# The output product of a hybrid decoder layer: half of its contraction as seven products of sums of blocks, two row blocks at a time

## The chip, the core and the metric

The kernel runs on one core of one Trainium2 chip. The metric is the device time of an execution in microseconds (us). A core has five engines that run side by side and wait for one another through semaphores: TensorE (PE, matmuls; PEld its weight loads), VectorE (DVE, V in the code), ScalarE (ACT, S), GpSimd (POOL, G) and SyncE (SP), which here issues every DMA. Operands lie in SBUF, matmuls write to PSUM, which has eight banks of 128 x 512 float32; the large arrays lie in HBM.

## The reference

One layer of inference for a prompt of 1024 tokens and 32 sample tokens (8 sequences of 4), width 1024, float32. What matters here is its end:

```python
u = jax.nn.sigmoid(gm) * (y_m @ w_mo) + jax.nn.sigmoid(ga) * (y_a @ w_ao)
x = x + gate * (u @ w_o)
...
y_prompt = rmsnorm(yp, g_final)     # the same for the 32 sample rows
```

`u @ w_o` is the output product: 1024 (and 32) rows, a contraction over 1024, 1024 columns. After it every row is scaled by its gate, added to the residual x, and normed by its mean square.

## The kernel before

The layer runs in stages: norm and gates of the input, the input projection (most of it already as seven products of sums of blocks, `block_products`), attention and the matrix memory beside it, and at the end three products: `att_out` (y_a by w_ao), `mem_out` (y_m by w_mo), and the output product.

**Splitting.** A float32 operand is split into a high part (a cast to the matmul's reduced float32, on ScalarE) and a low part (the difference, on VectorE or GpSimd). A product of two operands is three matmuls: high by high, high by low, low by high.

**The w_mo product.** `for d in range(KT)` runs eight steps; step d makes 128 of the 1024 columns of u for all tokens, in three pieces of 384, 384 and 288 tokens. The pieces go through four PSUM banks in turn (`banks`: pg, pg, pa, pa), and VectorE empties them: `tgw_mo` is gated, then added to u (for d of 6 and 7 by GpSimd). Beside step d two halves of row block d of w_out are loaded (`raw`, 128 x 512), and split into `wo_h[d, i]` and `wo_l[d, i]`: the cast on ScalarE, the low part of one half on VectorE, of the other on GpSimd. All 32 halves stay in SBUF. They come from the pool `half` (`ht`), of 43 buffers; raw loads come from the pool `wr` of nine.

**The output product.** The loop runs over the eight row blocks of 128 tokens. A block's u (eight pieces of 128 x 128) is split, and for each half of the columns 24 matmuls of 128 x 512 (8 parts of the contraction, three each) are summed in one PSUM bank. The eighth block does its second half as two quarters of 256 columns. `add_part` multiplies the bank by the gate (`gbc`), adds it to the residual row `xb`, and has ScalarE square it with a running sum; `last_norm` forms the factor of the rows with eleven or so small steps on VectorE (`recip_sqrt`: a bit trick and three iterations) and scales and stores the two halves.

**The sample rows.** The 32 sample rows would use a quarter of TensorE's columns; `sample_rows` therefore runs four parts of the contraction side by side, on the unsplit w_out, which is loaded once more, sixteen halves of 256 KB (`wos`). It is a generator that the loop over row blocks resumes: eight matmuls for each half of the contraction and each half of the columns, sixteen in a go, then three additions on VectorE.

**Storage at the end.** `gbc` (gates of the prompt), `gsb` (of the samples), `gf` (final gain) and the residual rows are eight tiles of 128 x 1024, `misc`, in two quarters of SBUF (`l0`, `l1`) that hold y_m until the last matmul of the w_mo product.

**Order.** The instructions are ordered for each engine by a scheduler at build time, which works through what is ready, by place in the program; PE's order is the program's. `Ordered` ties the instructions of VectorE and ScalarE to the order written while its `on` is set; it is off from the middle of the kernel to the end. SP's queue works in order: a DMA that waits for its buffer holds back those behind it.

Of the kernel before, what the change touches and what calls it, by code (L numbers as in the profile page):

```python
# [10 lines left out]
F32 = mybir.dt.float32  # L11
# [9 lines left out]
D = 1024  # L21
# [151 lines left out]
def body(tc, a):  # L173
    nc = tc.nc
    with ExitStack() as ctx:
# [5 lines left out]
        def pg(shape, name):  # L181
            return ps.tile(shape, F32, tag="g", bufs=2, name=name)
# [4 lines left out]
        def pb(shape, name):  # L187
            return ps.tile(shape, F32, tag="b", bufs=2, name=name)
# [51 lines left out]
        def dma(out, in_, late=False):  # L240
            stores(in_.tensor)
            issue(out, in_, late)
# [10 lines left out]
        def mm(out, lhsT, rhs, start, stop, share=1, more=False):  # L253
            n = int(np.prod(rhs.shape[1:]))
            side.now += max(n, 250) / 2400 if rhs.dtype == F32R else max(n * 4 // share, 128) / 2400
            side.products += 1
            in_order(nc.tensor.matmul(out, lhsT, rhs, start=start, stop=stop, skip_group_check=more))  # L257
# [6 lines left out]
        def recip_sqrt(half, shape, name):  # L264

            yi = sm(shape, name + "_y", 2)
            w = sm(shape, name + "_w", 2)
            V.tensor_scalar(yi.bitcast(I32), half.bitcast(I32), 1, None, op0=ALU.logical_shift_right)
            V.tensor_scalar(yi.bitcast(I32), yi.bitcast(I32), -1, -0x2108A621, op0=ALU.mult, op1=ALU.add)
            for _ in range(3):  # L270
                if shape[1] == 1:
                    V.scalar_tensor_tensor(w, yi, half, yi, op0=ALU.mult, op1=ALU.mult)
                else:
                    V.tensor_tensor(w, yi, yi, op=ALU.mult)
                    V.tensor_tensor(w, w, half, op=ALU.mult)
                V.scalar_tensor_tensor(yi, w, 1.5, yi, op0=ALU.subtract, op1=ALU.mult)
            return yi
# [1499 lines left out]
        wo_h, wo_l = {}, {}  # L1777
        for d in range(KT):
            mem_out(d, ymx, u)
            for i in range(2):  # L1780
                raw = raw_tile(f"wo{d}_{i}").rearrange("p k n -> p (k n)")
                dma(raw, a["w_out"][d * 128:(d + 1) * 128, HALF[i]], True)
                wo_h[d, i], wo_l[d, i] = (ht([128, 512], f"wo_{x}{d}", F32R) for x in "hl")
                S.copy(wo_h[d, i], raw)
                (G if i else V).tensor_tensor(wo_l[d, i], raw, wo_h[d, i].bitcast(F32), op=ALU.subtract)


        assert not due
# [12 lines left out]
        def add_part(xb, src, gb, n, cf, ss):  # L1801
            t = ht([128, 512], "fot")[:n, :cf.stop - cf.start]
            V.tensor_tensor(t, src, gb[:n, cf], op=ALU.mult)
            V.tensor_tensor(xb[:n, cf], xb[:n, cf], t, op=ALU.add)
            jk = ht([128, 512], "fjk", BF16)
            S.activation(jk[:n, :cf.stop - cf.start], xb[:n, cf], AF.Square, accum_out=ss)

        def last_norm(tb, xb, n, ss, parts):
            v = sm([128, 1], "fv", 2)
            V.tensor_scalar(v[:n], ss[:n, 0:1], 0.5 / D, 0.5 * EPS, op0=ALU.mult, op1=ALU.add)  # L1810
            for f in range(1, len(parts)):
                V.scalar_tensor_tensor(v[:n], ss[:n, f:f + 1], 0.5 / D, v[:n], op0=ALU.mult, op1=ALU.add)
            r = recip_sqrt(v[:n], [n, 1], f"fr{n}")
            yo = a["y_p"][tb * 128:tb * 128 + 128] if tb < 8 else a["y_s"]
            lo, hi = slice(0, 512), slice(512, D)
            if tb == 7:
                V.tensor_tensor(xb[:n, lo], xb[:n, lo], gf[:n, lo], op=ALU.mult)
                S.activation(xb[:n, lo], xb[:n, lo], AF.Copy, scale=r)
            else:
                V.scalar_tensor_tensor(xb[:n, lo], xb[:n, lo], r, gf[:n, lo], op0=ALU.mult, op1=ALU.mult)  # L1820
            dma(yo[:, lo], xb[:n, lo])
            V.scalar_tensor_tensor(xb[:n, hi], xb[:n, hi], r, gf[:n, hi], op0=ALU.mult, op1=ALU.mult)
            dma(yo[:, hi], xb[:n, hi])

        def sample_rows():
            xb = residual(8, NS)
            acc = [po([128, 512], f"fo8_{f}") for f in range(2)]
            for kq in range(0, KT, 4):
                raws = []
                for k in range(kq, kq + 4):  # L1830
                    for f in range(2):
                        raws.append(raw_tile(f"wos{k}{f}").rearrange("p k n -> p (k n)"))
                        dma(raws[-1], a["w_out"][k * 128:(k + 1) * 128, HALF[f]])
                yield
                for f in range(2):
                    for j in range(4):
                        mm(acc[f][32 * j:32 * j + 32], u(kq + j, SEQ, NS), raws[2 * j + f],
                           start=(kq == 0), stop=(kq > 0))
            ss = sm([128, 3], "fsss", 1)
            for f in range(2):  # L1840
                yield
                t = ht([128, 512], "fo8s")[:NS]
                S.copy(t, acc[f][0:32])
                for j in (32, 64, 96):
                    V.tensor_tensor(t, acc[f][j:j + 32], t, op=ALU.add)
                add_part(xb, t, gsb, NS, slice(f * 512, f * 512 + 512), ss[:NS, f:f + 1])
            last_norm(8, xb, NS, ss, (0, 1))

        rows8 = sample_rows()
        for tb in range(8):  # L1850
            if 2 <= tb < 7:
                next(rows8, None)
            t0 = tb * 128
            xb = residual(tb, 128)
            uh, ul = [], []
            for k in range(KT):
                if k % 4 == 0:
                    gh, gl = (granule(f"u{tb}{t}{k}", t, 4, F32R) for t in ("wh", "wl"))
                us = u(k, t0, 128)
                uh.append(gh[:, k % 4])  # L1860
                ul.append(gl[:, k % 4])
                S.copy(uh[k], us)
                V.tensor_tensor(ul[k], us, uh[k].bitcast(F32), op=ALU.subtract)
            ss = sm([128, 3], "fss", 2)
            parts = ((0, 512), (512, 256), (768, 256)) if tb == 7 else ((0, 512), (512, 512))
            for f, (p0, pn) in enumerate(parts):
                cf = slice(p0, p0 + pn)
                acc = pg([128, 512], f"fo{tb}_{f}")
                o = acc[:, :pn]
                for k in range(KT):  # L1870
                    mm(o, uh[k], wo_h[k, p0 // 512][:, p0 % 512:p0 % 512 + pn], start=(k == 0), stop=False)
                    mm(o, uh[k], wo_l[k, p0 // 512][:, p0 % 512:p0 % 512 + pn], start=False, stop=False)
                    mm(o, ul[k], wo_h[k, p0 // 512][:, p0 % 512:p0 % 512 + pn], start=False, stop=(k == KT - 1))
                add_part(xb, o, gbc, 128, cf, ss[:, f:f + 1])
            last_norm(tb, xb, 128, ss, parts)


OUTS = {
# [73 lines left out]
```

## Time and profile before

| | us |
|---|---|
| median of 3 runs | 854.86 (854.39 to 855.19) |
| the profiled execution | 853.27 |
| its span, first to last instruction | 851.1 |
| PE busy in the span | 830.6 (98%) |
| DVE, ACT, POOL busy | 566.5, 387.8, 41.8 |
| w_mo product on the chain | 705.15 to 751.6 |
| output product on the chain | 751.6 to 843.25 |

Times inside the kernel are counted from the start of the span. In the rows of a timeline stand the start, the length, the engine, the line, the operation, its result and its operands, and in brackets how long the engine had been idle and what released it. In the rows of groups stand the count, the busy time, the mean in ns, and the idle time ahead. In the rows of stretches stand the length and the busy time of PE, PEld, DVE, ACT and POOL with the number of instructions, then the granted clock of TensorE, the busy share of the DMA engines and GB/s. The granted clock is 0.998 of full speed over the run. Line 219 is the helper of `Ordered`, line 257 that of every matmul, and line 245 that of every DMA issue, so the groups are told apart by tiles: `fo` is the output product's bank, `u0wh` to `u7wl` are the split row blocks, `rows_l` the residual rows, `fot` the gated part, `fjk` the squares, `fr_y` and `fr_w` the norm's factor.

### The profile page before, as it was taken

The page shows a single profiled execution, that of the slowest core. Times are in us where ns is not written, and L with a number is a line of the kernel's source. Part 1 is how long each engine was busy: PE and PEld are TensorE (multiplying, and loading weights), DVE is VectorE, ACT ScalarE, POOL GpSimd, SP SyncE. Part 2 cuts the span into 40 slices and gives each one's busy share as a digit, 9 for nine tenths or more (in the row PEclk, how much of TensorE's full clock was granted, in tenths as well). Part 3 has the DMA queues.
Part 4 walks back from the last instruction along what each step waited for, and adds up shares of the span by engine and source line. Part 5 has one row for each costly group of instructions (what it writes and reads, how often), then busy time and mean ns, then how long its engine had stood idle before and what let it go on. Part 6 is the DMA issues. An engine that isn't in the chain of part 4 may idle for free.

```text
span 851.1 us, 15314 instructions
## 1 busy us (share of the span) xinstructions
PE 830.6 (98%) x5256; PEld 697.7 (82%) x5256; DVE 566.5 (67%) x1600; ACT 387.8 (46%) x989; POOL 41.8 (5%) x81
## 2 busy tenths in 40 slices
PE   6899999999999999999999999999999999999996
PEld 3689989789888988888888777777778999987785
DVE  3787785555666785656655656787877657746586
ACT  4672356546665564555444444444446232223231
POOL 0220000000000000000000000000002011220000
PEclk9999999999999999999999999999999999999999
DMA  9996549348537565273423453554435789353402
GB/s 324 365 360 187 144 142 293 107 118 288 193 102 234 167 187 169 84 223 95 134 97 110 133 135 105 150 165 125 125 113 178 276 277 305 123 161 113 172 25 80
DMA packets 114321, 146.48 MB, mean 172 GB/s; under 512 B 27089, under 2 KB 70993, under 8 KB 114213
## 3 DMA queue, kind: packets, MB, share of 16 engines
q1 hardware_dynamic: 114244, 145.52, 53.3%
q8 instruction: 41, 0.67, 0.3%
q14 instruction: 36, 0.29, 0.1%
HBM read 107.50 MB, written 38.99 MB: 172 GB/s over the span
## 4 chain that ended last, share of the span: by engine, by line
PE 93%; ACT 2%; DVE 2%; DMA 1%; issue 1%; SPq 0%; DVEq 0%; ACTq 0%
PE fo L257 11%; PE bx L257 11%; PE by L257 10%; PE bw L257 10%; PE g_aq L257 6%; PE g_w_mo L257 5%; PE bz L257 5%; PE g_w_ao L257 5%; PE g_mq L257 4%; PE g_mk L257 3%; PE g_mv L257 3%; PE smp L257 2%; PE sc L257 2%; PE oT L257 2%; PE pt L262 1%; PE g_ak L257 1%
## 5 line engine op out<-in xcount | busy, mean ns | idle before, releaser
L257 PE MATMUL g_w_ao<-ya,wh_w_ao 128*128 128x384 f32 (+1 forms) x192 | 45.6, 322 | 0.1
L257 PE MATMUL g_w_mo<-ym_l,wh_w_mo 128*128 128x384 f32 (+1 forms) x192 | 45.7, 323 | 0.0
L219 ACT ACTIVATE p<-p,nmx 128x256 f32<-128x256 f32 (+1 forms) x64 | 31.0, 487 | 20.6 <-DVE nmx L219 20.6
L219 ACT ACTIVATE fjk<-rows_l 128x512 bf16<-128x512 f32 (+2 forms) x19 | 11.6, 609 | 50.3 <-DVE rows_l L219 26.3
L219 DVE CUSTOM_DVE_ANT_0 p<-sc,cst,sink 128x256 f32<-128x256 f32 (+1 forms) x64 | 26.1, 464 | 12.2 <-PE sc L257 10.3
L257 PEld LDWEIGHTS g_w_ao<-ya,wh_w_ao 128*128 128x128 f32 x192 | 33.4, 188 | 0.6 <-DVE ya L219 0.4
L257 PEld LDWEIGHTS g_w_mo<-ym_l,wh_w_mo 128*128 128x128 f32 x192 | 33.5, 188 | 0.0
L257 PE MATMUL g_aq<-h_h,wh_aq 128*128 128x384 f32 (+1 forms) x96 | 32.5, 338 | 0.0
L257 PE MATMUL g_aq<-h_l,wh_aq 128*128 128x384 f32 (+1 forms) x96 | 31.0, 323 | 0.0
L257 PE MATMUL g_aq<-h_h,wl_aq 128*128 128x384 f32 (+1 forms) x96 | 31.0, 323 | 0.0
L257 PE MATMUL g_w_mo<-ym_l,wl_w_mo 128*128 128x384 f32 (+1 forms) x96 | 31.0, 323 | 0.0
L257 PE MATMUL g_w_ao<-ya,wl_w_ao 128*128 128x384 f32 (+1 forms) x96 | 30.8, 321 | 0.0
L257 PE MATMUL g_mk<-h_h,wh_mk 128*128 128x384 f32 (+1 forms) x72 | 24.9, 346 | 0.0
L257 PE MATMUL g_mq<-h_h,wh_mq 128*128 128x384 f32 (+1 forms) x72 | 24.8, 344 | 0.0
L257 PE MATMUL g_mk<-h_h,wl_mk 128*128 128x384 f32 (+1 forms) x72 | 23.2, 323 | 0.0
L257 PE MATMUL g_mk<-h_l,wh_mk 128*128 128x384 f32 (+1 forms) x72 | 23.2, 323 | 0.0
L257 PE MATMUL g_mq<-h_h,wl_mq 128*128 128x384 f32 (+1 forms) x72 | 23.2, 323 | 0.0
L257 PE MATMUL g_mq<-h_l,wh_mq 128*128 128x384 f32 (+1 forms) x72 | 23.2, 322 | 0.0
L219 DVE TENSOR_TENSOR fot<-fo,rows_l 128x512 f32<-128x512 f32 (+1 forms) x17 | 11.2, 657 | 15.1 <-PE fo L257 15.0
L257 PEld LDWEIGHTS g_aq<-h_h,wh_aq 128*128 128x128 f32 x96 | 18.0, 188 | 1.4 <-issue 1.0
L219 DVE SCALAR_TENSOR_TENSOR tgw_mo<-tgw_mo,g_w_mo 128x384 f32<-128x384 f32 (+1 forms) x24 | 12.5, 519 | 10.1 <-PE g_w_mo L257 10.1
L219 DVE SCALAR_TENSOR_TENSOR u_h<-tgw_ao,g_w_ao 128x384 f32<-128x384 f32 (+1 forms) x24 | 12.2, 517 | 9.4 <-PE g_w_ao L257 9.2
(1453 smaller groups left out, 2674.6 us busy)
## 6 DMA issues: line engine op xcount, KB each, us to landing
hb<-hD SPq DMA_DIRECT2D x24, 256.0 KB
x<-xT SPq DMA_DIRECT2D x16, 256.0 KB
early_h<-w_ada SPq DMA_DIRECT2D x8, 512.0 KB
hD<-x SPq DMA_DIRECT2D x16, 256.0 KB
adar_ga<-w_ada SPq DMA_DIRECT2D x16, 256.0 KB
wr_ga<-w SPq DMA_DIRECT2D x16, 256.0 KB
wr_gm<-w SPq DMA_DIRECT2D x16, 256.0 KB
taD<-gt SPq DMA_DIRECT2D x16, 256.0 KB
```

The source lines that it names most:

```text
L219: ins = f(*args, **kw)
L257: in_order(nc.tensor.matmul(out, lhsT, rhs, start=start, stop=stop, skip_group_check=more))
L262: in_order(nc.tensor.transpose(out, in_, idn))
```

## The change

The contraction of the output product is cut in two. Its first half (four parts of 128) is done, for two row blocks at a time, as seven products of sums of blocks: the rows' blocks are two row blocks by two halves of two parts, the weights' blocks two halves of two parts by two halves of the columns. The sums of the weights' blocks are formed and split beside the w_mo product (`out_sums`), those of u in the loop (`Rows.start`). The second half of the contraction stays as it was, block by block (`plain`), and is summed into the same banks. A bank X is copied on by ScalarE to W, and W to Y, so that a product which belongs to several results is made once; `copied` opens a bank that has not been opened with one matmul ahead of the copy. The weights need 22 splits instead of 16; seven of the low parts live in the pool `wr`.

The pairs of row blocks run one after another, with V, S and G in the order written. The norms of the two blocks of a pair are formed in one chain on columns of 2 (the last but one with the sample rows: 3), during the next pair. Products of the gate that don't read PSUM go to GpSimd (`gated_ahead`). In the last pair GpSimd multiplies rows by the final gain ahead, ScalarE scales rows, and product 4, product 7 and the plain part of one result are done in quarters of 256 columns.

The sample rows' weights are no longer loaded during the w_mo product, but four at a time into `misc[1]` (where `gsb` is loaded at the start, and again later) and `misc[7]`; the products come in groups of four instead of eight, and the last additions go to GpSimd.

```diff
-        V, S, G = Ordered(nc.vector, "V"), Ordered(nc.scalar, "S"), nc.gpsimd
+        V, S, G = Ordered(nc.vector, "V"), Ordered(nc.scalar, "S"), Ordered(nc.gpsimd, "G")
+        G.on = False
...
+        def out_split(name, t, eng):
+            wo[name].append(tuple(ht([128, 512], f"wo_{name}{x}", F32R) for x in "hl"))
+            hi, lo = wo[name][-1]
+            S.copy(hi, t)
+            eng.tensor_tensor(lo, t, hi.bitcast(F32), op=ALU.subtract)
+
+        def out_sums(k):
+
+            (b11, b12), (b21, b22) = held.pop(k), held.pop(k + 2)
+            out_split("b22", b22, G)
+            V.tensor_tensor(b22, b22, b12, op=ALU.subtract)
+            V.tensor_tensor(b12, b12, b11, op=ALU.subtract)
+            out_split("t1", b12, G)
+            V.tensor_tensor(b11, b11, b22, op=ALU.add)
+            out_split("b21", b21, G)
+            out_split("t3", b22, V)
+            V.tensor_tensor(b21, b21, b11, op=ALU.subtract)
+            out_split("t2", b11, G)
+            out_split("t4", b21, V)
+
+        for d, k in enumerate((0, 2, 1, 3, 4, 5, 6, 7)):
             mem_out(d, ymx, u)
...
+        def sample_rows():
+            raws = [misc[m][:, c] for m in (1, 7) for c in HALF]
+            acc = [po([128, 512], f"fo8_{f}") for f in range(2)]
+            sums = []
+
+            def load(f, kq):
+                for j in range(4):
+                    dma(raws[j], a["w_out"][(kq + j) * 128:(kq + j + 1) * 128, HALF[f]])
+
+            def products(f, kq):
+                for j in range(4):
+                    mm(acc[f][32 * j:32 * j + 32], u(kq + j, SEQ, NS), raws[j], start=(kq == 0), stop=(kq > 0), share=4)
+
+            load(0, 0)
+            yield
+            for f in range(2):
+                products(f, 0)
+                load(f, 4)
+                yield
+                products(f, 4)
...
+            def start(self, *ns):
+                (a1, p1), (a2, p2) = self.x
+                for n in ns:
+                    if n == 1:
...
+                        self.split(1, a1[:, 0:2], "A", 0)
+                        V.tensor_tensor(self.s, a2[:, 0:2], a2[:, 2:4], op=ALU.add)
+                    elif n == 5:
+                        self.split(5, self.s, "A", 2)
+                        V.tensor_tensor(a2[:, 0:2], a1[:, 0:2], a2[:, 0:2], op=ALU.subtract)
+                        V.tensor_tensor(a1[:, 0:2], self.s, a1[:, 0:2], op=ALU.subtract)
+                    elif n == 2:
+                        self.split(2, a1[:, 2:4], "B", 0)
+                        V.tensor_tensor(a1[:, 2:4], a1[:, 2:4], a1[:, 0:2], op=ALU.subtract)
...
+        def copied(src, name, pool=None, c=slice(0, 512), new=None):
+            t = ht([128, 512], name) if pool is None else pool([128, 512], name)[:, :c.stop - c.start]
+            if new:
+                mm(t, new.w[1][0][:, 0], wo["b11"][0][0][:, c], start=True, stop=True)
+            S.copy(t, src[:, c])
+            return t
+
+        def gated_ahead(xb, t, c):
+            G.tensor_tensor(t, t, gbc[:, c], op=ALU.mult)
+            G.tensor_tensor(xb[:, c], xb[:, c], t, op=ALU.add)
...
+        for i, r in enumerate(blocks_of_rows):
+            nxt = blocks_of_rows[i + 1] if i < 3 else None
+            aside = lambda *when: next(rows8, None) if i in when else None
+            before, xb, ss = (xb, ss), [residual(2 * i + c, 128) for c in range(2)], sm([128, 6], "fss", 2)
+            aside(0)
+            X, Z = pg([128, 512], "foX"), pa([128, 512], "foZ")
+            r.product(1, X, True)
+            W = copied(X, "foW", pg, new=r if i == 0 else None)
+            if i:
+                add_part(before[0][1], Y[0], gbc, 128, lo, None)
+            aside(1, 2)
+            r.product(5, Z, True)
+            p5 = copied(Z, "fop5")
+            gated_ahead(xb[0], p5, hi)
+            aside(2)
+            r.start("p2", 7, 3)
...
+            r.product(2, X, False)
+            r.plain(0, 0, X)
+            r.product(6, W, False)
+            parts = ((0, 512),) if nxt else ((0, 256), (256, 256))
+            Y = [copied(W, f"foY{c0}", pb if c0 else pa, slice(c0, c0 + n), r if c0 or i == 0 else None) for c0, n in parts]
+            r.start(4)
+            add_part(xb[0], X, gbc, 128, lo, None if nxt else ss[:, 0:1])
+            if nxt:
+                nxt.start(1, 5)
+            if i:
+                rs = norm_rows(before[1], 2 if nxt else 3, 2)
+            r.plain(1, 1, Z, range(2))
...
+            if nxt:
+                seventh()
+                gated_ahead(xb[1], y7, hi)
+                aside(0, 1)
+                r.plain(1, 1, Z, range(2, 4))
+                add_part(xb[1], Z, gbc, 128, hi, None, V, G)
+                for c in range(2) if i else ():
+                    rows_out(2 * i - 2 + c, before[0][c], rs[:, c:c + 1])
+                first_row()
+                aside(0, 1)
+                nxt.start("p1")
+                r.product(4, Y[0], False)
+                r.plain(1, 0, Y[0])
             else:
...
+                first_row()
+                seventh()
+                square(xb[0][:, hi], ss[:, 1:2])
+                gated_ahead(xb[1], y7, hi)
+                for c, (tb, x, _) in enumerate(done):
+                    rows_out(tb, x, rs[:, c:c + 1], S)
+                rs = norm_rows(ss, 1, 2)
+                final_gain(xb[0])
+                r.plain(1, 1, Z, range(2, 4))
+                add_part(xb[1], Z, gbc, 128, hi, ss[:, 2:3])
+                final_gain(xb[1], 128, (hi,))
+                for f, (y, (c0, n)) in enumerate(zip(Y, parts)):
+                    r.product(4, y, False, c0, n)
+                    r.plain(1, 0, y, range(4), c0, n)
+                    add_part(xb[1], y, gbc, 128, slice(c0, c0 + n), ss[:, f + 3:f + 4])
+                rows_out(6, xb[0], rs, S)
+        rows_out(7, xb[1], norm_rows(ss[:, 2:5], 1, 3), S)
```

More of the change, by code (lines that the diff above doesn't have):

```diff
@@ L1799, in residual, with add_part @@
             return xb
-        def add_part(xb, src, gb, n, cf, ss):
+        def add_part(xb, src, gb, n, cf, ss, mult=V, add=V):
             t = ht([128, 512], "fot")[:n, :cf.stop - cf.start]
[L1803 to L1818, printed above, removed]
-            else:
[L1820 to L1875, printed above, removed]
@@ new lines, in add_part, with norm_rows @@
+            mult.tensor_tensor(t, src, gb[:n, cf], op=ALU.mult)
+            add.tensor_tensor(xb[:n, cf], xb[:n, cf], t, op=ALU.add)
+            if ss is not None:
+                square(xb[:n, cf], ss)
+        def norm_rows(ss, m, parts):
+            v = sm([128, 3], "fv", 2)[:, :m]
+            sums = ss[:, :m * parts].rearrange("p (m f) -> p m f", f=parts)
+            V.tensor_scalar(v, sums[:, :, 0], 0.5 / D, 0.5 * EPS, op0=ALU.mult, op1=ALU.add)
+            for f in range(1, parts):
+                V.scalar_tensor_tensor(v, sums[:, :, f], 0.5 / D, v, op0=ALU.mult, op1=ALU.add)
+            return recip_sqrt(v, [128, m], f"fr{m}")
@@ new lines, in square @@
+        def square(x, ss):
+            S.activation(pb([128, 512], "sq")[:x.shape[0], :x.shape[1]], x, AF.Square, accum_out=ss)
+        def sample_rows():
[15 more added lines that the diff above has]
+                products(f, 4)
+                sums.append(raw_tile("fo8s").rearrange("p k n -> p (k n)")[:NS])
+                S.copy(sums[f], acc[f][0:32])
+                if f == 0:
+                    load(1, 0)
+                else:
+                    dma(gsb[:NS], gsD)
+                    xb = residual(8, NS)
+                yield
+                for j in (32, 64, 96):
+                    V.tensor_tensor(sums[f], acc[f][j:j + 32], sums[f], op=ALU.add)
+                yield
+            for f in range(2):
+                add_part(xb, sums[f], gsb, NS, HALF[f], None, G, G)
+            row8.append(xb)
@@ new lines, in copied @@
+        def copied(src, name, pool=None, c=slice(0, 512), new=None):
[7 more added lines that the diff above has]
+            G.tensor_tensor(xb[:, c], xb[:, c], t, op=ALU.add)
+        rows8 = sample_rows()
```

90 lines of the change are left out of this document (83 added, 7 removed).

## The prediction

> **What bounds the kernel now.** I read the page first (busy times, then the chain), then the chain in order of time for the end, then TensorE's timeline inside the output product, and last the queues beside it.
>
> ```profile
> PE 830.6 (98%) x5256; PEld 697.7 (82%) x5256; DVE 566.5 (67%) x1600; ACT 387.8 (46%) x989; POOL 41.8 (5%) x81
> ...
> 705.15 46.45 PE g_w_mo L257 x288
> 751.59 91.65 PE fo L257 x440
> ...
> 844.19 0.52 ACT fjk L219 x2
> ...
> 844.73 0.17 DVE fv L219
> ...
> 846.64 0.72 ACT L219 ACTIVATE rows_l<-rows_l,fr_y 128x512 f32<-128x512 f32 x1 [1.95 <-DVE fr_y L219]
> ```
>
> The reader is to see that TensorE (PE) is the chain without a hole through the w_mo product (705.15 on) and the output product (751.59 to 843.25), and that behind it stand 7.9 us of norm and store, to the span's end at 851.1. So a matmul taken out of the output product is worth its pitch, as long as the operands of the next one are there. The pitch is read between starts, since a matmul's own 0.39 us overlaps the next:
>
> ```profile
> 776.64 0.39 PE L257 MATMUL fo<-wo_h,u2wh 128*128 128x512 f32 x1
> ...
> 783.89 0.39 PE L257 MATMUL fo<-wo_h,u2wl 128*128 128x512 f32 x1
> 784.21 1.92 PE L257 MATMUL fo<-wos,u_h 128*32 128x512 f32 x16
> 786.07 0.50 PE L257 MATMUL fo<-wo_h,u3wh 128*128 128x512 f32 x1
> 786.41 0.40 PE L257 MATMUL fo<-wo_l,u3wh 128*128 128x512 f32 x1
> ...
> 837.32 0.28 PE L257 MATMUL fo<-wo_h,u7wh 128*128 128x256 f32 x1
> ...
> 842.95 0.28 PE L257 MATMUL fo<-wo_h,u7wl 128*128 128x256 f32 x1
> ```
>
> The first two rows are 32 steps apart: 7.25/32 = 0.2266 us for 512 columns. The last two are 47 steps apart: 0.120 us for 256. Between them stands one group of the sample rows' products: from 784.12 (one pitch after 783.89) to 786.07.
>
> [...]
>
> **The change, part by part: matmuls.** Before, two row blocks take 2 x 2 x 8 x 3 = 96 matmuls. After, the first half of the contraction takes 7 products x 2 x 3 = 42 and the second half 2 x 2 x 4 x 3 = 48: 90. Four pairs save 24, and 24 x 0.2266 = 5.44 us. Those of 256 columns in the last pair are 12 + 12 + 24 = 48, as before. `copied` adds fills where a bank has not been opened: two of 512 columns in the first pair, one of 256 in the last: 2 x 0.2266 + 0.12 = 0.57 us. The sample rows' 16 products come in four groups instead of two. Entering cost 784.21 - 784.12 = 0.09 us and leaving 0.34 - 0.23 = 0.11, so two more groups cost 0.4 us. TensorE's sum is -5.44 + 0.57 + 0.4 = -4.47 us, all on the path.
>
> **New waits inside a pair: costed at nothing.** A product is only 6 matmuls now, 1.36 us. Copying X to W lies under product 5, copying W to Y under six matmuls of the plain half.
>
> ```profile
> L219 ACT COPY bw<-bx x16: 570/580/597, 287.2 to 640.0; 128x512 f32<-128x512 f32 x16
> L219 ACT ACTIVATE fjk<-rows_l 128x512 bf16<-128x512 f32 x15 | 9.5, 632 | 40.1 <-issue 23.1 <-DVE rows_l L219 16.1 <-ACT fjk L219 0.9
> L219 ACT ACTIVATION_READ_ACCUMULATOR fjk<-rows_l 128x1 f32 x17 | 3.2, 187 | 0.0
> ```
>
> The copy takes 0.58 us (0.16 of drain before it), so 0.6 us are to spare, if ScalarE is free. Ahead of the copy to Y stand p5, the splits of p2, 7 and 3 (two more of 0.6 in width) and four squares of 0.63 whose sums are read in 0.19, partly overlapped: 0.6 + 1.5 + 4 x 0.63 to 0.82, 4.6 to 5.4 us, in a stretch of 24 matmuls, 5.4 us. The cover is thin: where it fails, each us that ScalarE is late beyond 0.6 is a us on PE, at most 1 in each of three pairs.
>
> **VectorE and GpSimd in a pair.** The units:
>
> ```profile
> L219 DVE TENSOR_TENSOR rows_l<-rows_l,fot 128x512 f32<-128x512 f32 x15 | 10.3, 688 | 1.0 <-DMA rows_l<-x_prompt 0.8
> L219 DVE TENSOR_TENSOR rows_l<-rows_l,fot 128x256 f32<-128x256 f32 x2 | 0.8, 422 | 0.0
> L219 DVE SCALAR_TENSOR_TENSOR rows_l<-rows_l,fr_y,rows_l 128x512 f32<-128x512 f32 x11 | 7.8, 749 | 0.2
> L1785 POOL TENSOR_TENSOR wo_l<-wo,wo_h 128x512 fp32r<-128x512 f32 x8 | 10.6, 1323 | 65.0 <-DVE wo_l L219 34.1 <-ACT wo_h L219 21.7 <-DVE wl_w_mo L219 4.6
> L219 DVE TENSOR_TENSOR fo8s<-fo,fo8s 32x512 f32<-32x512 f32 x6 | 4.1, 686 | 0.2
> 707.87 1.30 POOL L1785 TENSOR_TENSOR wo_l<-wo,wo_h 128x512 fp32r<-128x512 f32 x1 [5.52 <-ACT wo_h L219]
> 707.88 1.71 DVE L219 TENSOR_TENSOR u_h<-u_h,tgw_mo 128x384 f32<-128x384 f32 x1
> ...
> 710.68 0.56 DVE L219 TENSOR_TENSOR u_h<-u_h,tgw_mo 128x384 f32<-128x384 f32 x1
> 751.40:843.25 91.85, 91.83 (x442) 73.98 (x440) 63.46 (x194) 25.33 (x90) 1.20 (x2) 1.00 0.36 122
> ```
>
> Low parts: 7 x 0.42 + 2 x 0.69 = 4.3 us. Sums of blocks: 4 x 0.42 = 1.7. Parts added to the rows: 7 x 0.69 = 4.8. One norm chain for two blocks instead of two: 13 small steps at about 0.2 us (nine of them took from 844.90 to 846.64), 2.5. Four scaled halves: 3.0. That is 16.3 us against 90 x 0.2266 = 20.4 us of PE, and in pairs 1 and 2 three additions for the samples, 2.1 us, more. The tightest thing V must deliver is the addition that frees W's bank for the next pair: in V's order it ends about 19 us into a pair, and PE needs it about 22 us in (the next pair's product 1, then the copy). I cost it at nothing; with those 3 us gone it is the slower rival below. The shorter norm chains save V's time and nothing on the path.
>
> **The w_mo product.** The formed blocks are split there: V gets 18 subtractions and sums instead of 8 (+10 x 0.69 = 6.9 us), ACT 22 casts instead of 16, GpSimd 12 subtractions instead of 8 (+4 x 1.32).
>
> ```profile
> 705.15:722.60 17.45, 17.45 (x110) 17.45 (x110) 13.57 (x24) 5.23 (x10) 3.89 (x3) 1.00 0.93 323
> 722.60:734.00 11.40, 11.40 (x72) 11.40 (x71) 8.39 (x17) 3.19 (x6) 2.59 (x2) 1.00 0.43 138
> 734.00:751.40 17.40, 17.40 (x110) 17.40 (x109) 10.91 (x27) 3.94 (x14) 5.99 (x6) 1.00 0.19 62
> 722.61 15.41 SPq L245 DMA_DIRECT2D wos<-w_out  x9
> ```
>
> The columns after the length are busy PE, PEld, DVE, ACT, POOL. V is idle for 3.9 + 3.0 + 6.5 = 13.4 us, enough for 6.9, and PE runs up to three pieces (46.45/24 = 1.94 us each) ahead of the evacuation. Cost nothing, at worst 2.5 us if the first stretch takes most of it. The sample rows' loads (wos) leave this stretch, and SP's queue with it.
>
> **The moved loads.** This is where I expect time to be given back. Before, eight of the sixteen sample loads (256 KB) have come by 738; now the first four are issued in the output stage, into two tiles of the `rows` storage that the w_mo product holds until its end, beside all that is loaded there anyway:
>
> ```profile
> 751.49 0.33 SPq L245 DMA_DIRECT2D rows_l<-x_prompt  x1
> 751.91 0.38 SPq L245 DMA_DIRECT2D rows_l<-gbD  x1
> 752.35 0.42 SPq L245 DMA_DIRECT2D rows_l<-g_final  x1
> 752.82 0.42 SPq L245 DMA_DIRECT2D rows_l<-gsD  x1
> ...
> 753.77 0.47 SPq L245 DMA_DIRECT2D rows_l<-x_sample  x1
> 754.29 1.20 SPq L245 DMA_DIRECT2D rows_l<-x_prompt  x2
> ...
> 761.70 0.69 DVE L219 TENSOR_TENSOR rows_l<-rows_l,fot 128x512 f32<-128x512 f32 x1 [0.81 <-DMA rows_l<-x_prompt]
> 751.40:764.10 12.70, 12.70 (x58) 10.51 (x57) 5.68 (x15) 3.32 (x14) 1.20 (x2) 1.00 0.86 269
> 764.00:765.00 1.00, 1.00 (x6) 0.84 (x5) 0.88 (x4) 0.70 (x2) 0.00 (x0) 1.00 0.07 20
> ```
>
> Now 3.42 MB (12.7 us x 269 GB/s) pass until 764.1, and a block needed early came at 761.7. After, x_sample's 0.13 MB is gone and 1.05 MB is added. Two of the four loads go over `gsb`, whose own load they must see landed first; behind SP's wait for it stands whatever SP issues later. If the two x_prompt of the next pair (1.05 MB) go before them, the four are complete after 4.33 MB, 0.92/0.287 = 3.2 us after 764.1, at 767.3; if not, after 3.28 MB, at 763.6. PE comes to the products `products(0, 0)` after 48 matmuls and two fills, 751.5 + 50 x 0.2266 = 762.8, with the first ones' slower start about 763.0. So PE waits 0.6 to 4.3 us, and every later matmul stands behind it. Program order speaks for the short end; that SP issued the first x_prompt ahead of gbD, which comes earlier in the program, shows a queue that lets what is ready pass, and speaks for the long end. I take 2.0. The second four must land within 24 matmuls, 5.4 us: four issues at 0.45, overlapped by 1.05/0.287 = 3.7 us of transfer, and about 1 us to start: 4.7, cost nothing, at worst 1 us. The pairs' stores are issued behind them.
>
> **The end.** Same chain for the last block: multiply, add, square, nine small steps, scale, store. ScalarE squeezes the sixth block's two scalings (about 0.72 us each) between the last square (844.71) and the scale (846.64): 1.44 in 1.93. GpSimd has 11 steps of 1.32 in the last pair and must multiply the last half by the gain before the scale. Bounds 0 to 1.5 us; I take 0.4, since all of it fits by the count, but with little room.
>
> **Sum.** -4.47 + 2.0 + 0.4 = -2.07 us. The profiled execution took 853.27 us (span 851.1 and 2.2 around it): 851.2. The median of the three runs is 1.59 above the profiled one: 854.86 - 2.07 = 852.8.
>
> **Rivals.** *The cover holds*: the loads are there by 763, or PE is late itself. For it: 763.6 is the lower bound. Then -4.47 + 0.4 = -4.1 and 850.8.
>
> *VectorE and GpSimd block each other* (ends slower). The rows at 707.87 and 707.88 show it: V's addition of two operands in SBUF took 1.71 us instead of 0.56 (710.68), as long as GpSimd's subtraction beside it lasted. In the output stage POOL was busy for 1.20 us; now it gets 5 steps of 1.32 = 6.6 us a pair. If V loses each whole step, a pair costs V 16.3 + 6.6 = 22.9 us, with samples 25.0. Pair 1 offers 20.4 and two sample groups of 1.1, 22.7; pair 2 offers 20.4. V falls behind by 2.3 and by 4.6, and PE stands still from the point at which the 3 us of slack are used up: 6.9 - 3.0 = 3.9 us. -2.07 + 3.9 = +1.8, 856.7. Against it: V's steps that read PSUM or are small, some 5 us a pair, were slowed by no row here, and GpSimd's steps may fall beside those.
>
> [...]
>
> *The loads are late at both places*: 4.3 us at the first, 0.6 more over the later ones: -4.47 + 4.9 + 0.4 = +0.8, 855.7.
>
> **How the numbers follow.** Forecast 0.42 (its own range by the wait's bounds, -4.47 + 0.6 + 0.4 to -4.47 + 4.3 + 0.4: 851.4 to 855.1); cover holds 0.20; blocked VectorE 0.23; late at both places 0.15. A difference of 0.2%, 1.7 us, is about what a measurement of this kernel can tell from none. Faster by more: the covered case's 0.20 and 0.29 of the forecast's 0.42 (a wait under 2.4 us), together 0.49. Within: the other 0.13 and 0.11 of the late loads, 0.24. Slower: 0.23 + 0.04 = 0.27. The range goes from a little below the covered case, 850.3, to a little above the blocked one, 857.8.
>
> **What would show it.** Right: 24 fewer fo matmuls at 0.2266; one hole of 1 to 4 us on PE before the first `fo8_0` group, ended by a DMA of w_out; no other hole over 1 us before the last; 8 us from the last matmul to the end. Wrong: holes at product 2 or 7 ended by ACT (thin cover), or ended by DVE with V steps of 1 us and more beside POOL; holes before 751; a tail over 9 us.

## The result, and the profile after

| | before | after |
|---|---|---|
| median, us (runs) | 854.39 (5; 853.54 to 855.19) | 862.08 (5; 861.19 to 863.72) |
| ratio | | 1.0091, 95% interval 1.0076 to 1.0105 |
| profiled execution, us (its span) | 853.27 (851.1) | 861.19 (859.4) |
| output product on TensorE | 751.43 to 843.07: 91.64 | 751.29 to 846.91: 95.62 |
| tail: from there to the end of the span | 8.03 | 12.49 |

Here and below the product is counted from the start of its first matmul to 0.12 us, one pitch of 256 columns, behind the start of its last.

The kernel became slower by 7.7 us, 0.9%; the forecast was 852.8. The product grew by 3.98 us and the tail by 4.46, and it began 0.14 earlier: together the 8.3 us of the span.

The page of the changed kernel, its busy times:

```profile
PE 829.9 (97%) x5235; PEld 694.6 (81%) x5235; DVE 589.8 (69%) x1551; ACT 403.5 (47%) x993; POOL 95.4 (11%) x118
```

VectorE (DVE) has 49 instructions fewer than before and is busy 23 us longer. GpSimd (POOL) has more than doubled. TensorE's timeline in the output product of the changed kernel (start, length, engine, operation; in brackets the idle time before it and what ended it; line 258 is now the helper of every matmul):

```profile
751.29 0.40 PE L258 MATMUL foX<-wo_b11h,u0whA 128*128 128x512 f32 x1
...
763.30 1.06 PE L258 MATMUL fo<-rows_l,u_h 128*32 128x512 f32 x6
765.01 1.05 PE L258 MATMUL fo<-rows_l,u_h 128*32 128x512 f32 x2 [0.65 <-DMA rows_l<-w_out]
765.99 0.50 PE L258 MATMUL foZ<-wo_h,u0whD 128*128 128x512 f32 x1
...
822.99 0.39 PE L258 MATMUL foZ<-wo_t1h,u3wlA 128*128 128x512 f32 x1
827.03 0.50 PE L258 MATMUL foX<-wo_b21h,u3whB 128*128 128x512 f32 x1 [3.65 <-ACT foW L219]
827.37 0.39 PE L258 MATMUL foX<-wo_b21l,u3whB 128*128 128x512 f32 x1
827.60 0.57 PE L258 MATMUL foX<-wo_b21h,u3wlB 128*128 128x512 f32 x1
...
830.95 0.45 PE L258 MATMUL foX<-wo_l,u3whC 128*128 128x512 f32 x1
...
846.79 0.28 PE L258 MATMUL foY<-wo_h,u3wlD 128*128 128x256 f32 x1
```

The reader is to see one large hole, a stretch in which TensorE stands idle, at product 2 of the last pair (3.65 us; 4.04 from start to start against 0.2266, so 3.81 lost), and eight matmuls behind it at (830.95 - 827.60)/8 = 0.42 us instead of 0.2266: another 1.5. The row names ScalarE's copy of X to W; who held that copy is in ScalarE's, VectorE's and GpSimd's timelines of the same kernel:

```profile
826.41 0.57 ACT L219 COPY foW<-foX 128x512 f32<-128x512 f32 x1 [7.98 <-DVE fot L219]
...
814.91 1.85 DVE L219 TENSOR_TENSOR u_h<-u_h 128x256 f32<-128x256 f32 x2
816.68 1.25 DVE L219 TENSOR_SCALAR fv<-fss 128x2 f32<-128x2 f32 x1
817.97 0.16 DVE L219 SCALAR_TENSOR_TENSOR fv<-fss,fv 128x2 f32<-128x2 f32 x1
...
820.22 0.69 DVE L219 TENSOR_TENSOR fot<-foZ,rows_l 128x512 f32<-128x512 f32 x1
820.83 3.76 DVE L219 SCALAR_TENSOR_TENSOR rows_l<-rows_l,fr_y,rows_l 128x512 f32<-128x512 f32 x4
...
825.63 0.68 DVE L219 TENSOR_TENSOR fot<-foW,rows_l 128x512 f32<-128x512 f32 x1
...
815.10 1.38 POOL L219 TENSOR_TENSOR foy<-foy,rows_l 128x512 f32<-128x512 f32 x1 [1.63 <-ACT foy L219]
816.55 1.36 POOL L219 TENSOR_TENSOR rows_l<-rows_l,foy 128x512 f32<-128x512 f32 x1
```

The copy waited 7.98 us for `fot<-foW`, VectorE's multiplication that frees W's bank. VectorE came to it late, with no idle time ahead of any row shown: two block sums took 1.85 instead of 0.88 and a step on a 128x2 column 1.25 instead of 0.16, with a GpSimd step of 1.36 to 1.38 beside each of the long ones. The same groups of VectorE's instructions, by line and form, in the output stage of the changed kernel, and then in the first experiment, which has the same VectorE instructions and no GpSimd work (busy us, mean ns of one):

```profile
L219 DVE TENSOR_TENSOR rows_l<-rows_l,fot 128x512 f32<-128x512 f32 x12 | 9.9, 827 | 0.5
L219 DVE TENSOR_TENSOR uwlE<-u_h,uwhE 128x256 fp32r<-128x256 f32 x8 | 7.4, 961 | 0.0
L219 DVE SCALAR_TENSOR_TENSOR rows_l<-rows_l,fr_y,rows_l 128x512 f32<-128x512 f32 x7 | 5.9, 890 | 0.0
L219 DVE TENSOR_TENSOR fot<-foX,rows_l 128x512 f32<-128x512 f32 x4 | 2.7, 685 | 0.1
```

```profile
L219 DVE TENSOR_TENSOR rows_l<-rows_l,fot 128x512 f32<-128x512 f32 x12 | 8.3, 692 | 0.4
L219 DVE TENSOR_TENSOR uwlE<-u_h,uwhE 128x256 fp32r<-128x256 f32 x8 | 3.0, 420 | 0.0
L219 DVE SCALAR_TENSOR_TENSOR rows_l<-rows_l,fr_y,rows_l 128x512 f32<-128x512 f32 x7 | 4.9, 748 | 0.0
L219 DVE TENSOR_TENSOR fot<-foX,rows_l 128x512 f32<-128x512 f32 x4 | 2.8, 688 | 0.1
```

The groups that read only SBUF are stretched (the second, 961 against 420 ns); the one that reads PSUM is not (685 against 688).

### The profile page after: what moved, and what is told of

The parts are those of the page before. It is cut to its first block, busy times and chain, and to the rows that moved or that the text cites. A ratio compares the mean times of both kernels' runs of the same rounds, so it can differ in the third digit from the quotient of the medians.

```text
span 859.4 us, 15300 instructions
## 1 busy us (share of the span) xinstructions
PE 829.9 (97%) x5235; PEld 694.6 (81%) x5235; DVE 589.8 (69%) x1551; ACT 403.5 (47%) x993; POOL 95.4 (11%) x118
## 5 line engine op out<-in xcount | busy, mean ns | idle before, releaser
L258 PEld LDWEIGHTS g_aq<-h_l,wh_aq 128*128 128x128 f32 x96 | 18.1, 188 | 0.0
L258 PEld LDWEIGHTS g_aq<-h_h,wl_aq 128*128 128x128 f32 x96 | 18.0, 188 | 0.0
```

## The experiments

In two of the profiled executions below (e2, e5) an earlier stretch that no experiment touches lost some 4 us, so that the output product began at 755.3; in the other runs from e1 to v9, but for v3 and v4, it began at 751.3 to 753.3. Stages are therefore compared by their length, times by the medians.

**GpSimd left out, or its work given to VectorE.** Theory A: a GpSimd step holds VectorE up. Theory B: VectorE has too much work of its own.

```
e1:  gated_ahead, final_gain, add_part(.., G, G), add_part(.., V, G): the G steps are dropped
e2:  G.tensor_tensor(..)  ->  V.tensor_tensor(..)   in the same places
```

> Leaves out all that GpSimd computes in the output stage: the gated products 5 and 7, the addition of Z to the second block, the sample rows' gain and addition, the final gains. VectorE's own steps and TensorE's stay as they are. Theory A (GpSimd blocks VectorE): VectorE's steps in SBUF go back to 0.42, 0.69 and 0.15 us, it gains about 7 us in the third pair, the hole of 3.65 us at product 2 of the last pair and the slow matmuls behind it (1.7 us) go, the tail of 12.3 us falls to 8 to 9; time 852 to 854. Theory B (VectorE has too much work of its own whatever GpSimd does; norm chain and scaled halves ahead of the addition that frees W's bank): the hole stays at 3 us or more, 860 to 862.

Measured: 851.02 us, ratio 0.9966 (0.9953 to 0.9979), a microsecond below the forecast of theory A. The hole and the slow matmuls are gone; product 89.69, tail 8.04. The steps left out are needed for the result, so this time is a bound and not a version.

> All that GpSimd computed in the output stage is done by VectorE, at the same places in the order. Theory A (blocked): VectorE loses about 7 us to GpSimd's nine steps in the third pair and gets nine steps of 0.69 = 6.2 us in their place, so nearly nothing changes: hole 2.5 to 4 us, time 859 to 863. Theory B (load alone, GpSimd costs VectorE nothing): VectorE has 3.5 us more in the second pair and 6.2 us more in the third, the hole grows to 8 us or more, time 867 to 872.

Measured: 860.08 us, ratio 1.0072 (1.0053 to 1.0091); no hole at product 2, product 91.74, tail 13.49. The time lies in theory A's range, but neither theory's hole came: TensorE waited twice for VectorE earlier, 0.82 and 0.69 us, and the tail became the longest so far. Busy times of e1 and e2:

```profile
PE 827.6 (97%) x5235; PEld 693.2 (82%) x5235; DVE 568.6 (67%) x1551; ACT 403.0 (47%) x993; POOL 49.2 (6%) x86
```

```profile
PE 830.0 (96%) x5235; PEld 694.3 (81%) x5235; DVE 588.1 (68%) x1583; ACT 403.3 (47%) x993; POOL 49.6 (6%) x86
```

Theory A holds for what a GpSimd step costs. The 32 steps on GpSimd (46.2 us of its time) lengthened VectorE's unchanged 1551 steps by 589.8 - 568.6 = 21.2 us, 0.66 a step; done by VectorE they cost it 588.1 - 568.6 = 19.5 us, 0.61 a step. Handing them to GpSimd relieved VectorE of nothing. VectorE's own load counts too, as theory B has it: e2 has no such blocking and is slower than before. With the 32 steps on neither engine the kernel is 3 us faster than before.

**Another order.** The scaled halves of the finished rows go behind W's addition.

```
-                for c in range(2) if i else ():
-                    rows_out(2 * i - 2 + c, before[0][c], rs[:, c:c + 1])
                 first_row()
                 ...
                 r.plain(1, 0, Y[0])
+                for c in range(2) if i else ():
+                    rows_out(2 * i - 2 + c, before[0][c], rs[:, c:c + 1])
```

> The four scaled halves of the pair before (3.0 to 3.8 us of VectorE) go from ahead of the addition that frees W's bank to the end of the pair; nothing else is changed. If VectorE's lateness at that one addition makes the hole (theory A and B both): it comes 3.8 us earlier, the hole of 3.65 us shrinks to under 0.5, the clock behind it stays full, and PE ends about 5 us earlier; with the tail as it is, 856 to 858. Rival (what is late is the backlog as a whole, and it only moves): a hole of 2 us or more comes back at another bank or at the copy to Y in the last pair, or the tail grows by as much; 860 or more.

Measured: 865.57 us, ratio 1.0131 (1.0116 to 1.0146). TensorE's timeline of e3:

```profile
825.52 0.50 PE L258 MATMUL foX<-wo_b21h,u3whB 128*128 128x512 f32 x1 [1.50 <-ACT foW L219]
...
836.95 0.58 PE L258 MATMUL foY<-wo_b11h,u3whA 128*128 128x256 f32 x1 [5.69 <-ACT sq L219]
837.33 0.63 PE L258 MATMUL foZ<-wo_h,u3whD 128*128 128x512 f32 x1
837.75 0.63 PE L258 MATMUL foZ<-wo_l,u3whD 128*128 128x512 f32 x1
```

The rival was right. The hole shrank to 1.5 us, and one of 5.69 opened at the copy to Y: later halves mean later stores and a later load of block 6; GpSimd's addition of product 5 waits for that load, its `memset` of the sums stands behind it, ScalarE's squares (`sq`) behind the `memset`, and the copy to Y behind the squares.

**The load of the sample weights.** `dma(gsb[:NS], gsD)` at the stage's start is left out; it is loaded again later.

> The first of the two loads of the sample gate rows at the stage's start is left out (it is loaded again before its use). If the second sample product group's wait of about 1.1 us is SP's wait for that load before w_out goes over it: wait under 0.4 us, 0.7 to 1.1 us less. If it is the amount of bytes ahead of it: wait about 0.9, nothing changes in the time.

Measured: 860.61 us, a single run. TensorE's timeline of e4:

```profile
763.30 1.07 PE L258 MATMUL fo<-rows_l,u_h 128*32 128x512 f32 x8
764.30 0.50 PE L258 MATMUL foZ<-wo_h,u0whD 128*128 128x512 f32 x1
...
825.94 0.80 PE L258 MATMUL foX<-wo_b21h,u3whB 128*128 128x512 f32 x1 [4.02 <-ACT foW L219]
```

SP's first four issues of the sample weights, in the changed kernel and then in e4:

```profile
753.63 6.96 SPq L246 DMA_DIRECT2D rows_l<-w_out  x4
...
753.15 2.44 SPq L246 DMA_DIRECT2D rows_l<-w_out  x4
```

The wait is gone (next product at 764.30 instead of 765.99, 1.69 us), and SP's four issues take 2.44 us instead of 6.96, so SP's wait for that load was its cause. The product is no shorter for it (95.70 us): the next sample group took 0.6 more, the hole grew from 3.65 to 4.02, since TensorE came earlier and VectorE did not, and the slow matmuls behind the hole went on for longer.

**The last pair alone.** `gated_ahead` and `final_gain` return at once for `i == 3`.

> Leaves out GpSimd's thirteen steps of the last pair alone (gated products 5 and 7, final gains); the first three pairs are as after. Theory A (a GpSimd step beside VectorE's costs up to its own length, in the tail as in the pairs): the hole at product 2 of the last pair and the slow matmuls behind it stay (3.5 to 4.1 and 1.6 us), the tail falls from 12.3 to 8.5 to 9.5; time 858 to 859.5. Rival (the tail is VectorE's backlog from the pairs before and the hole, whatever GpSimd does at the end): tail 11 us or more, 861 or more.

Measured: 858.86 us, ratio 1.0061 (1.0044 to 1.0078); hole 4.04 us, tail 8.07, a little below theory A's range. So the 4.4 us of the tail belong to GpSimd's thirteen steps of the last pair.

**The hole filled.**

```
+            if i == 3:
+                fill = po([128, 512], "fill")
+                for _ in range(16):
+                    mm(fill, r.w[1][0][:, 0], wo["b11"][0][0], start=True, stop=True)
             r.product(2, X, False)
```

> Adds sixteen matmuls of 512 columns, whose result nobody reads, between product 5 and product 2 of the last pair, where TensorE stood for 3.65 us: it waits as long but is not idle (16 x 0.2266 = 3.63 us). If the eight matmuls at a pitch of 0.43 us behind the hole are slow because of the idleness itself (the granted clock falls after it): they run at 0.2266, the granted clock stays at 1.00, TensorE ends about 1.6 us earlier; time 860 to 861 if VectorE can follow. If they are slow for what runs beside them (DMA, ScalarE's squares into PSUM): they stay at 0.43 and the time is 862 or more.

Measured: 862.31 us, ratio 1.0097 (1.0083 to 1.0111). TensorE's timeline, then VectorE's, of e6:

```profile
823.92 3.79 PE L258 MATMUL fill<-wo_b11h,u3whA 128*128 128x512 f32 x16
828.11 0.50 PE L258 MATMUL foX<-wo_b21h,u3whB 128*128 128x512 f32 x1 [0.40 <-ACT foW L219]
828.44 0.40 PE L258 MATMUL foX<-wo_b21l,u3whB 128*128 128x512 f32 x1
828.68 0.39 PE L258 MATMUL foX<-wo_b21h,u3wlB 128*128 128x512 f32 x1
828.91 0.40 PE L258 MATMUL foX<-wo_b21h,u3whB 128*128 128x512 f32 x1
```

```profile
837.01 1.26 DVE L219 TENSOR_SCALAR fv<-fss 128x3 f32<-128x3 f32 x1
838.30 1.20 DVE L219 SCALAR_TENSOR_TENSOR fv<-fss,fv 128x3 f32<-128x3 f32 x1
839.53 1.22 DVE L219 TENSOR_SCALAR fr_y<-fv 128x3 int32<-128x3 int32 x1
...
841.38 1.26 DVE L219 SCALAR_TENSOR_TENSOR fr_y<-fr_w,fr_y 128x3 f32<-128x3 f32 x1
...
842.87 1.15 DVE L219 TENSOR_TENSOR fr_w<-fr_w,fv 128x3 f32<-128x3 f32 x1
...
844.05 1.21 DVE L219 SCALAR_TENSOR_TENSOR fr_y<-fr_w,fr_y 128x3 f32<-128x3 f32 x1
```

The matmuls behind run at full speed (0.23 us): idleness made them slow. The product became 1.78 us shorter (93.84), and the tail took it all and more, 14.91 us. Six steps of the norm chain, 0.16 us each alone, now met a GpSimd step each and took 1.15 to 1.26: the end is VectorE's, not TensorE's.

**Versions without GpSimd in the output stage.** v3 multiplies the gate into `w_out` beforehand (16 GpSimd steps, written to DRAM and read back), so that a part is added in one VectorE step; v4 places these steps later.

> The gate is multiplied into w_out once, by GpSimd in the middle of the kernel (sixteen steps, 4 MB written to DRAM and read back in place of w_out), so that a part is added to its row in one step of VectorE from PSUM; GpSimd has nothing left in the output stage, its two additions of products 5 and 7 go to VectorE; the sample gate rows are loaded once; the scaled halves are one step a row; the last pair's norm chain of block 6 comes after Z. Theory A: a pair costs VectorE 4.3 + 1.7 + 4 x 0.69 + 2 x 0.69 + 2.6 + 2 x 1.25 = 15.3 us without blocking against 20.4, no hole over 0.5 us is left and the tail is 8 to 9: TensorE 751.3 + 87.9, tail 8.5, and 1.8 around the span: 849.5, range 848 to 851. Rival: sixteen GpSimd steps and 8 MB more in the middle block VectorE and SP there: the output product starts 2 to 5 us later, 852 to 855.

> As v3_gate_in_weights, but the sixteen multiplications of w_out by the gate begin some 95 us later, behind the stretch in which they made TensorE wait (250 to 400 us), with 14 us instead of 9 between a load and its use, and in the last pair the norm chain and the three rows of the pair before are done by VectorE ahead of its additions, where it stood idle for 3.4 us. If the 10.5 us that v3 lost before the output product came from where and how tightly the steps were placed: output product begins at 751 to 753, 88.5 us long, tail 8 to 8.7: 849 to 852. Rival (sixteen GpSimd steps cost VectorE and TensorE as much wherever they stand): begins at 757 or later, 856 or more.

Measured: v3 861.35 us (1.0085; 1.0072 to 1.0099), v4 860.75 (1.0080; 1.0062 to 1.0098). First and last matmul of the product in v3:

```profile
761.75 0.40 PE L258 MATMUL foX<-wo_b11h,u0whA 128*128 128x512 f32 x1
...
850.14 0.28 PE L258 MATMUL foY<-wo_h,u3wlD 128*128 128x256 f32 x1
```

Where VectorE has room the stage does nearly as forecast: 88.5 us and no hole but 0.22, tail 9.34 (v4: 88.48 and 8.54). But the product begins 10.5 us later (v4: 10.8): the rival was right at both places, in v3 with twice the loss it named, and the gain is paid in the middle. In v4 two holes of TensorE there, 3.54 us (to 379.02) and 2.78 (to 528.31, where the changed kernel has 1.20), and the half clock behind them come to about the 10.8: 5.1 us more of idle time, and half of the 11.5 us in which TensorE worked at half its clock. Which GpSimd step or load caused them was not taken apart.

v5 to v9 leave the gate where it is and take steps from VectorE:

```
v5:  e2 and e4; a finished row scaled in one step of 1024 columns; rows 4, 5, 8 ahead of X's addition
v6:  W + p5 and Z + y7 first, then the gate: 3 steps instead of 4 for a half
v6b: four sample strips summed in two steps instead of three
v7:  squares of rows 4 and 8 ahead of product 5's copy
v8:  Newton steps of the norm chains on ScalarE, but for block 7
v9:  rows 4, 5, 8 again by VectorE, row 8 behind W's addition
```

> As e2_all_on_vector (nothing on GpSimd in the output stage, gate still multiplied there by VectorE), with the sample gate rows loaded once, the scaled halves done as one step a row, rows 4, 5 and 8 without a separate gain, and the last pair's order of v4. If what is left in e2 is VectorE's load and order (about 20 us a pair against 20.4): no hole over 1 us, tail 9 to 11 instead of 13.5: 854 to 857, above v4 by the price of the sixteen multiplications that stay. Rival (order alone does it): 850 to 852 like v4.

> As v5_all_on_vector_ordered, but the copies of products 5 and 7 are added to W and Z before the gate (one step from PSUM) instead of being gated and added to the row on their own: 3 steps instead of 4 for each of these halves, 2 x 0.69 = 1.4 us of VectorE less in each pair. If VectorE's load is what is left in v5 (no idle time of it from 790 us on): its lateness at the end falls by up to 4 us, TensorE's part 89.5 to 90, tail 10.8 to between 8.5 and 9.5, time 852 to 853.5, below the kernel before. Rival (what is left is the order of the last additions and the norm chain): tail 10.5, 855.

> As v6_products_added_first, and the four strips of the sample product are added in two steps (64 rows, then 32) instead of three: 0.69 us of VectorE less in the second and in the third pair. By VectorE's load: up to 1 us less than v6, 851.5 to 853. Rival (VectorE is no longer behind in v6): the same as v6.

> As v6b_two_sample_sums, but in the last pair ScalarE squares the finished rows 4 and 8 right behind the copy of X to W, ahead of the copy of product 5 and the casts, and copies product 7 ahead of the squares of block 6. In v6b VectorE stood idle for 1.8 us there, waiting for these squares, and worked without a gap from there to the end. If VectorE's time from the last pair's middle to the end sets the tail: 1 to 1.8 us less, tail 9 to 9.9, time 852 to 853. Rival (the tail waits for something that stands later, such as the scaling of block 6 ahead of the last norm chain): less than 0.5 us.

> As v7_squares_first, but the nine Newton steps of the reciprocal root are done by ScalarE, one column at a time (Square, Identity with scale and bias, Copy with scale), for all rows but block 7; VectorE keeps the two steps of the sum and the two of the first guess. In the last pair the scaled rows 4, 5 and 8 come behind W's addition. VectorE loses 9 x 0.2 = 1.8 us in the second, third and last pair and 1.3 us at block 6; ScalarE gains 18 to 27 steps of about 0.2 us a pair. If VectorE's load is what holds the tail at 10.8 to 11 us since GpSimd was taken off (8.0 in e1_no_gpsimd): tail 8.3 to 9.5, time 851.5 to 853. Rival (ScalarE, in order, takes its place: copies of W, Y and product 7 come late, or the rows wait for its chain): holes on TensorE ended by ScalarE, or tail over 10.5, 854 or more.

> As v8_norm_on_scalar, but in the last pair the norm chain of rows 4, 5 and 8 is VectorE's again, the scaled rows 4 and 5 come right behind it and row 8 behind W's addition, where VectorE stood idle for 2.85 and 0.9 us in v8; only block 6's chain stays with ScalarE there. If the tail is VectorE's work after those idle times (3.7 us of it lay between W and Z in v8): TensorE's part 88.5, tail 9.5 to 10.2, time 852 to 853.5. Rival (ScalarE, in order, holds VectorE or TensorE back as soon as it has a chain): tail over 11, 855 or more.

| | median | ratio to before, 95% | product | tail |
|---|---|---|---|---|
| v5 | 855.62 | 1.0017 (1.0006 to 1.0027) | 90.26 | 10.84 |
| v6 | 854.52 | 0.9996 (0.9986 to 1.0005) | 89.12 | 10.84 |
| v6b | 853.88 | 0.9996 (0.9988 to 1.0005) | 88.83 | 10.87 |
| v7 | 854.03 | 0.9995 (0.9984 to 1.0006) | 88.72 | 10.99 |
| v8 | 856.00 | 1.0022 (1.0010 to 1.0034) | 88.45 | 12.78 |
| v9 | 853.09 | 0.9986 (0.9976 to 0.9996) | 88.30 | 10.23 |

v5 came as expected. v6 shortened the product and not the tail, and missed its forecast by a microsecond, as its rival has it; v6b and v7 changed nothing that can be told, as their rivals have it, which speaks for a tail set by VectorE's last stretch. v8's rival was right by its number: VectorE stood idle for 2.85 us ahead of W and then had 3.7 us of scaled rows between W and Z. v9 mended that and is faster than both kernels, by 0.14% over the one before; the interval nearly reaches no difference, and v9 is the best of six variants. VectorE's timeline of v9 at the end:

```profile
842.93 0.42 DVE L219 TENSOR_TENSOR rows_l<-rows_l,fot 128x256 f32<-128x256 f32 x1
843.27 1.28 DVE L219 SCALAR_TENSOR_TENSOR rows_l<-rows_l,fr_y,rows_l 128x1024 f32<-128x1024 f32 x1
844.47 0.14 DVE L219 TENSOR_SCALAR fv<-fss 128x1 f32<-128x1 f32 x1
```

TensorE ended at 841.17 and the last addition 2.2 us later (1.1 in e1), and block 6's scaling, 1.2, stands between it and block 7's norm chain: together these are the 2.2 us by which the tail is still above e1's 8.04. Whether another order closes it was not tried.

## Why the prediction was wrong, point by point

- **Matmuls, -4.47**: right in kind. e1's product of 89.69, without its load wait (1.69) and the first pair's wait for W (0.38 from start to start), is 87.62: 4.02 less than before. The four sample groups of eight take 1.20 us each with their edges, against 2.06 for one of sixteen: 0.7 more and not 0.4.
- **Copies at nothing**: right but for 0.38 us in the first pair (a hole of 0.22). The hole that ends with ScalarE's copy is VectorE's.
- **The w_mo product at nothing**: right; the output product began 0.14 us earlier.
- **Moved loads, 2.0 (0.6 to 4.3)**: 1.69, and for the reason given, a wait for the load of `gsb` (e4). The later loads, put at nothing, cost 0.4: the fourth sample group waited for its weights.
- **VectorE and GpSimd at nothing, "3 us of slack"**: this is the step that failed. VectorE's work in a pair was added up as if GpSimd's steps beside it were free. The row of 1.71 us beside 0.56 was read and the blocking was made a rival at 0.23, against which stood that some of VectorE's steps read PSUM or are small. The first half is so (685 ns); the second is not: small steps are held longest in proportion (1.25 us for 0.16). From e1 the blocking costs 0.66 us a step, half of GpSimd's length, and that is enough, since VectorE was busy for 9.55, 9.65 and 9.05 of each 10 us from 790 to 820. The 3 us of slack were not there either where it mattered: in e1, without blocking, W's bank is free 3.5 us before ScalarE copies into it in the third pair, but only 1.0 us before in the last.
- **The rival's own sum**: its mechanism and its place, the addition that frees W's bank, were right, and its hole of 3.9 us measured 3.81. That the size fits so well is partly luck: it counted five steps of GpSimd in each of two pairs at their whole length, 6.6 us a pair, against 3.0 of slack. Against e1, VectorE's steps in the changed kernel are 4.9 us longer between its first and second addition that frees W's bank (five GpSimd steps) and 7.3 between its second and third (nine, the four of the sample rows among them). Its time, 856.7, was 5.4 us short, for two costs that were in no sum: the slow matmuls behind the hole (1.5) and the tail.
- **The end, 0.4 (0 to 1.5)**: 4.5, the second term that failed. The GpSimd steps were counted against GpSimd's own time and not against VectorE's; without them (e5, e1) the tail is 8.0 to 8.1, as before the change.

The sum with measured terms: -4.0 (matmuls) + 0.4 (first pair) + 1.7 and 0.4 (loads) + 3.8 (hole) + 1.5 (slow matmuls) + 4.5 (tail) - 0.1 = 8.2 of the 8.3 us of the span.

## What to carry to other kernels

Beside a VectorE that was busy without a pause a GpSimd step was no help here: it cost VectorE 0.66 us (e1) for 0.61 saved (e2). When matmuls are taken out of a stage that TensorE bounds, add up the other engines' work against the shorter stage, blocking included, before the gain is believed; and look for the step whose lateness stops TensorE, since moving it moved the hole here to the next bank (5.69 us in e3). A wait on TensorE of 2 us or more between two matmuls had a second price in slower matmuls in every run listed below: 1.5 us behind the 3.65 us of the changed kernel.

## What the runs showed of the hardware

- After the long holes of these runs TensorE ran at half its clock for a while. In the changed kernel, a window of the stretch behind the hole of 3.65 us (busy PE, PEld, DVE, ACT, POOL, then the granted clock):

```profile
827.40:831.00 3.60, 3.60 (x11) 2.82 (x10) 3.56 (x5) 3.60 (x12) 2.93 (x2) 0.54 0.66 246
```

  The granted clock was 0.50 for 3.4 us there, and for 6.8 us after the holes of 4.02 (e4), 4.04 (e5) and 5.69 us (e3). Shorter holes did the same ahead of the output product: 2.06 us (e5) and 2.42 (e2) with 3.4 us of half clock, 1.98 (v3, with 1.39 close behind), 2.78 and 3.54 (v4) with 6.8. The hole of 1.75 us in e6 did not, nor the one of 1.20 (to 520.34) in the changed kernel, nor the hole that was filled (0.40 us left of it). TensorE's timeline of v4 behind the hole of 2.78 us, and a window of it:

```profile
528.31 0.80 PE L258 MATMUL bx<-h_h,wh_pquery_gate__6218 128*128 128x512 f32 x1 [2.78 <-ACT gt L219]
...
529.33 0.63 PE L258 MATMUL bx<-h_h,wl_pquery_gate__6219 128*128 128x512 f32 x1
529.76 0.63 PE L258 MATMUL bx<-h_h,wh_pquery_gate__6218 128*128 128x512 f32 x1
...
529.00:530.00 1.00, 1.00 (x4) 0.81 (x3) 0.94 (x3) 0.46 (x1) 0.00 (x0) 0.50 0.67 262
```

  Three pitches of the changed kernel from 829.25 to 830.53 were 0.427 us each, against 0.2266 at a granted clock of 1.00. Holes from 1.98 us (v3) on were enough, and the stay at 0.50 was 3.4 us or twice that.
- A step of VectorE with one SBUF input (`fv`, a `tensor_scalar` on 128x2) was held too: 1.25 us beside a GpSimd step of 1.36 in the changed kernel, 0.16 in e1.
- GpSimd's steps on 32 rows took 1.35 to 2.07 us in the changed kernel, no less than those on 128 rows and as many columns (1.26 to 1.78).
- On a single column ScalarE's Identity with a bias and a scale read from SBUF took 0.38 us and its Copy with such a scale 0.28, where VectorE's steps took 0.16 to 0.22 (v8): the chain of a block takes longer there.
